# Two more pairs of gate tiles in seven products, and an earlier place for two copies and one load

## The chip, the cores and the metric

The kernel runs on one core of a Trainium2 chip. The metric is device time in microseconds (us) of one execution; smaller is better. A core has five instruction queues that run side by side: TensorE (PE in the profile, with PEld for its weight loads), VectorE (DVE), ScalarE (ACT), GpSimd (POOL) and SyncE (SP, which here only issues DMAs). Each queue runs its instructions in the order in which the program gives them to it, and waits at an instruction until what it needs is there.

## The reference, cut to what matters

Two layers over 512 tokens of width 1024, ahead of which 16 learned tokens are put. In float32:

```
h = RMSNorm(x)
[u_pool | z_pool | c_q | c_kv | k_rope | z_mla | g_pool | g_mla] = h @ W_in    # 512,512,768,256,32,512,1024,1024 columns
y_pool = W_pool_up( PoolMix(u_pool) * silu(z_pool) )      # four groups: mean of the last 2, 4, 8, 16, then 128x128 weights a group
y_mla  = W_mla_up( MLA(c_q, c_kv, k_rope) * silu(z_mla) ) # causal attention, 8 heads
x = x + W_out( sigmoid(g_pool) * y_pool + sigmoid(g_mla) * y_mla )
```

g_pool and g_mla are 1024 columns each: eight output tiles of 128, called gp and gm here. After the second layer the 16 learned tokens are dropped, so that layer computes its gates for 512 tokens only.

## The kernel before, in words

**Data and precision.** Activations lie transposed, channels on the 128 partitions and tokens along the free dimension. Each float32 operand is split in a high and a low part, and each product is three matmuls, high x high (line L192 of the profile), low x high (L195) and high x low (L196), into one PSUM bank. Output tile m of a product with 1024 inputs is 8 blocks of 128 rows, so 24 matmuls; its weights are two half tiles of 128x512 (256 KB). Each half tile is fetched by SP into one of three buffers `raw` (L115); ScalarE copies the high part (`whi`, L187) and VectorE subtracts to get the low part (`wlo`, L188), each into one of three buffers. So three half tiles are in flight at a time.

**Seven products for eight.** In the second layer the pairs gp0 to gp3 are computed as a 2x2 block product with seven products for eight (a scheme of Strassen's kind): the blocks are the two output tiles, two halves of 512 inputs and two halves of 256 tokens. Sums of the four blocks of weights are made ahead, during the first layer, by DMA: SP copies a half tile into DRAM (`weight_sums`, L356), and POOL adds others onto it by accumulating DMAs (L359). Sums of the activations (`mixed`) are made once. `fast` runs the products in the order 1, 6, 7, 5, 2, 4, 3, each with 4 blocks x 3 matmuls of 256 columns, and VectorE combines them (`fast` L632 to L647). `got_gp` then takes the gate's tanh on ScalarE and multiplies the pooled values by it on VectorE. The other gates, gm0 to gm7, go through `add` as plain products of 512 columns; `ev_gate` takes their tanh, and a DMA puts them into DRAM (`gate`). The output product W_out uses seven products as well (`out_pairs`, L1092 on): there product 6 adds onto the PSUM bank of product 1, so it waits until ScalarE has carried product 1 away (`carry`, L1163); POOL adds that to x by an accumulating DMA.

**What sets the order.** A list `plan` holds the matmul work that fills the gaps of the attention heads. A generator `stream` emits it, and fetches a half tile's weights when their predecessors are three tiles ahead. `fill` advances the plan by FILL ns of matmul time for each gap (2950 in the first layer, 2700 in the second) until the name in RESERVE is reached; what is left runs after the heads. `after(ns, f)` calls f when the plan's clock has come so far. A scheduler then orders each engine's instructions; `behind(a, b)` makes it put a behind b. The pooled groups' weights (128x512, `wgr`) are planned after `v`, fetched into a `raw` buffer like the rest, and split by `split` into the two `sv` buffers (L303 and L304).

**The change and the prediction's steps touch** `wload`, `weight_sums`, `fast`, `got_gp`, `carry`, the plan, and the constants FILL and RESERVE.

## Time and profile before

| what | us |
|---|---|
| median of 3 runs (781.44 to 783.92) | 782.54 |
| the profiled execution | 781.9 |
| its span | 780.1 |
| TensorE busy | 773.2 |
| VectorE busy | 569.7 |
| ScalarE busy | 444.7 |
| POOL busy | 232.7 |
| granted TensorE clock | 1.00 |

Engine rows read: start, length, engine, line, operation, outputs <- inputs, shape, count; in square brackets how long the engine had been idle, and what released it. Group rows give the busy time, the mean of one in ns, and the idle time of the engine ahead of the group. The stretch from 608 to 690 us lies in the second layer's heads. Idle time of an engine that TensorE does not wait for costs nothing.

### The profile page before, as it was taken

The page shows a single profiled execution, that of the slowest core. Times are in us where ns is not written, and L with a number is a line of the kernel's source. Part 1 is how long each engine was busy: PE and PEld are TensorE (multiplying, and loading weights), DVE is VectorE, ACT ScalarE, POOL GpSimd, SP SyncE. Part 2 cuts the span into 40 slices and gives each one's busy share as a digit, 9 for nine tenths or more (in the row PEclk, how much of TensorE's full clock was granted, in tenths as well). Part 3 has the DMA queues.
Part 4 walks back from the last instruction along what each step waited for, and adds up shares of the span by engine and source line. Part 5 has one row for each costly group of instructions (what it writes and reads, how often), then busy time and mean ns, then how long its engine had stood idle before and what let it go on. Part 6 is the DMA issues. An engine that isn't in the chain of part 4 may idle for free.

```text
span 780.1 us, 15325 instructions
## 1 busy us (share of the span) xinstructions
PE 773.2 (99%) x5469; PEld 710.9 (91%) x5469; DVE 569.7 (73%) x1326; ACT 444.7 (57%) x1016; POOL 232.7 (30%) x303
## 2 busy tenths in 40 slices
PE   9999999999999999999999999999999999999998
PEld 8999899999999999999997898887788999988887
DVE  5848787446778876589764577866897888864994
ACT  7645555645566665645564446546657766664552
POOL 1024525103335333211330136221006625340213
PEclk9999999999999999999999999999999999999999
DMA  6232457765646465565662424425557666662645
GB/s 245 82 96 89 125 171 151 177 168 144 156 110 164 116 141 120 156 156 184 169 171 82 109 75 122 133 62 178 146 132 167 173 187 158 175 226 72 210 137 154
DMA packets 65325, 112.92 MB, mean 145 GB/s; under 512 B 10704, under 2 KB 15696, under 8 KB 65248
## 3 DMA queue, kind: packets, MB, share of 16 engines
q1 hardware_dynamic: 55344, 92.18, 39.1%
q0 software_dynamic: 8896, 17.92, 12.9%
q10 hardware_dynamic: 1008, 1.84, 0.7%
q8 instruction: 43, 0.70, 0.4%
q14 instruction: 34, 0.28, 0.1%
HBM read 100.18 MB, written 22.62 MB: 157 GB/s over the span
## 4 chain that ended last, share of the span: by engine, by line
PE 91%; DVE 4%; DMA 2%; ACT 1%; issue 1%; POOL 0%; DVEq 0%; ACTq 0%; POOLq 0%
PE mm L192 26%; PE mm L196 26%; PE mm L195 25%; PE S L195 3%; PE S L196 3%; PE S L192 3%; PE mm L979 2%; DVE wlo L188 1%; PE o L985 1%; PE o L984 1%; PE S L506 1%; DMA raw<-wgr 1%; DMA xb<-xT 1%; PE mm L408 1%; ACT whi L187 0%
## 5 line engine op out<-in xcount | busy, mean ns | idle before, releaser
L192 PE MATMUL mm<-hh,whi 128*128 128x264 f32 (+2 forms) x992 | 306.2, 311 | 0.5 <-DVE u L550 0.4
L196 PE MATMUL mm<-hh,wlo 128*128 128x264 f32 (+2 forms) x992 | 304.4, 309 | 0.1
L195 PE MATMUL mm<-hl,whi 128*128 128x264 f32 (+2 forms) x992 | 304.1, 308 | 0.0
L188 DVE TENSOR_TENSOR wlo<-raw,whi 128x512 fp32r<-128x512 f32 (+1 forms) x253 | 180.0, 714 | 100.3 <-ACT whi L187 98.0
L187 ACT ACTIVATE whi<-raw 128x512 fp32r<-128x512 f32 (+1 forms) x253 | 154.2, 613 | 168.7 <-PE mm L195 110.2
L192 PEld LDWEIGHTS mm<-hh,whi 128*128 128x128 f32 x992 | 186.2, 188 | 11.3 <-issue 1.0
L195 PEld LDWEIGHTS mm<-hl,whi 128*128 128x128 f32 x992 | 186.8, 188 | 8.7
L196 PEld LDWEIGHTS mm<-hh,wlo 128*128 128x128 f32 x992 | 185.9, 188 | 9.0 <-DVE wlo L188 0.6
L922 POOL TENSOR_SCALAR pa<-pa,rs 128x272 f32<-128x272 f32 (+1 forms) x32 | 33.2, 1038 | 103.3 <-DVE rs L941 64.5
L922 POOL TENSOR_SCALAR cq<-cq,rs 128x400 f32<-128x400 f32 (+1 forms) x32 | 51.2, 1600 | 0.0
L192 PE MATMUL mm<-cq,whi 128*128 128x264 f32 (+2 forms) x140 | 43.8, 313 | 0.0
L195 PE MATMUL mm<-cq,whi 128*128 128x264 f32 (+2 forms) x140 | 43.7, 312 | 0.0
L196 PE MATMUL mm<-cq,wlo 128*128 128x264 f32 (+2 forms) x140 | 43.3, 312 | 0.1
L908 DVE CUSTOM_DVE_ANT_0 S<-S,maskw,nqs 128x272 f32<-128x272 f32 (+4 forms) x80 | 38.6, 498 | 5.3 <-PE S L196 5.0
L725 POOL TENSOR_TENSOR racc<-racc,tmp 128x264 f32<-128x264 f32 (+1 forms) x15 | 14.0, 936 | 85.5 <-ACT tmp L724 85.5
L304 DVE TENSOR_TENSOR tl<-mm,th 128x512 fp32r<-128x512 f32 (+1 forms) x64 | 30.0, 483 | 8.0 <-ACT th L303 6.3
L359 POOL DMA_DIRECT2D wsum<-wout x8 | 7.0, 875 | 91.6 <-PE mm L196 86.9
L303 ACT ACTIVATE th<-mm 128x512 fp32r<-128x512 f32 (+1 forms) x64 | 26.3, 433 | 10.2 <-PE mm L979 9.6
L915 ACT ACTIVATE cq<-S,bia 128x400 f32<-128x400 f32 (+2 forms) x48 | 24.5, 514 | 13.2 <-DVE bia L953 8.5
L192 PE MATMUL mm<-u,whi 128*128 128x264 f32 (+1 forms) x96 | 31.3, 326 | 0.0
L196 PE MATMUL mm<-u,wlo 128*128 128x264 f32 (+1 forms) x96 | 30.9, 322 | 0.0
L195 PE MATMUL mm<-kn,whi 128*128 128x264 f32 (+1 forms) x96 | 30.6, 320 | 0.0
(344 smaller groups left out, 1684.7 us busy)
## 6 DMA issues: line engine op xcount, KB each, us to landing
raw<-win SPq DMA_DIRECT2D x139, 256.0 KB, 2.8
raw<-wout SPq DMA_DIRECT2D x22, 256.0 KB, 3.6
bc<-kdr SPq DMA_DIRECT2D x16, 264.0 KB, 4.5
wsum<-wout SPq DMA_DIRECT2D x16, 256.0 KB, 3.5
raw<-wpu SPq DMA_DIRECT2D x16, 256.0 KB, 2.7
wsumgp<-win SPq DMA_DIRECT2D x16, 256.0 KB, 3.4
raw<-wmu SPq DMA_DIRECT2D x16, 256.0 KB, 2.8
raw<-wsumgp SPq DMA_DIRECT2D x16, 256.0 KB, 4.3
```

What stands on the lines that cost most here:

```text
L187: act.activation(hi[:, :n], raw[:, :n], AF.Copy)
L188: dve.tensor_sub(lo[:, :n], raw[:, :n], hi[:, :n].bitcast(F32))
L192: first = pe.matmul(out, wh, xh, start=start, stop=False, skip_group_check=more)
L195: pe.matmul(out, wh, xl, start=False, stop=False, skip_group_check=more)
L196: newest[0] = pe.matmul(out, wl, xh, start=False, stop=stop, skip_group_check=more)
L303: act.activation(hi[:, a:b], src, AF.Copy)
L304: dve.tensor_sub(lo[:, a:b], src, hi[:, a:b].bitcast(F32))
L725: self.acc_last = gp.tensor_add(self.acc[:, a:b], self.acc[:, a:b], t[:, :b - a])
L908: dve.tensor_tensor_reduce(out=sv, in0=sv, in1=mask, scale=nqs[:, i, h:h + 1], scalar=3e38, op0=ALU.add, op1=ALU.min, accum_out=bia[:, c:c ...
L915: act.activation(pv, sv, AF.Exp, scale=-1.0, bias=bia[:, i:i + 1], accum_out=rs[:, c:c + 1])
L922: gp.tensor_scalar(pt[i], pt[i], rs[:, i:i + 1], None, op0=ALU.mult)
L979: pe.transpose(tr[:, P * (i - j):P * (i - j + 1)], pt[i][:, NM + P * j:NM + P * (j + 1)], ident)
```

## The change

Three things are done, beside constants.

1. Of layer 1's eight gm tiles, gm2 with gm3 and gm4 with gm5 become the pairs gq1 and gq2, by `fast`, with the weight sums `wsum["gm"]`, which are made like those of gp: eight steps a pair in the first layer, 64 instead of 48, 3100 ns apart instead of 3850. `got_gm` takes the tanh of each 256-token half on ScalarE and sends each half to DRAM by a DMA of ScalarE's own queue. The order of layer 1's gates was gm0, gm1, gp0, gm2, gp1, gm3, gp2, gm4, gp3, gm5, gm6, gm7; it is gm0, gm1, gp0, gq1, gp1, gp2, gq2, gp3, gm6, gm7. FILL of layer 1 goes from 2700 to 2640, RESERVE from gm5 to gp3.
2. After a carry is emitted, the second and the third weight copy that follow it in the program (`urgent`) are put behind it on ScalarE.
3. The pooled groups' weights are fetched into a buffer `bc` of their own kind, not into `raw`, and are planned after `u2`, not after `v`.

```
-FILL = (2950.0, 2700.0)
-RESERVE = ("gm5", "gm5")
+FILL = (2950.0, 2640.0)
+RESERVE = ("gm5", "gp3")
...
     loads = [0]
+    urgent = []
 
     def wload(src, n, gain, spare, buf=None, held=False):
+        if held:
+            hi, lo = slot("sv", F32R, bufs=2), slot("sv", F32R, bufs=2)
+            raw = slot("bc", bufs=3)
+            sp.dma_start(raw[:, :n], src)
+            split(hi, lo, raw[:, :n], 0, n)
+            return hi, lo
...
-        if held:
-            hi, lo = slot("sv", F32R, bufs=2), slot("sv", F32R, bufs=2)
-            split(hi, lo, raw[:, :n], 0, n)
-            return hi, lo
...
-        act.activation(hi[:, :n], raw[:, :n], AF.Copy)
+        made = act.activation(hi[:, :n], raw[:, :n], AF.Copy)
+        for e in urgent:
+            e[1] += 1
+            if 1 < e[1] < 4:
+                behind(made, e[0])
...
-    def weight_sums(name, w):
+    def weight_sums(name, w, u0=0):
...
-        def fast(self, name, a, b, u, got):
+        def fast(self, name, a, b, s, u, got):
             order = (1, 6, 7, 5, 2, 4, 3)
-            s = wsum["gp"][u]
...
+        def got_gm(self, m, s, v, t):
+            if self.gms[m] is None:
+                self.gms[m] = slot("ts" if m % 2 else "tc")
+            d = self.gms[m][:, s[0]:s[1]]
+            act.activation(d, v, AF.Tanh, scale=0.5)
+            act.dma_start(gate[:, m, s[0] - NM:s[1] - NM], d)
...
-                act.activation(t, v, AF.Copy, scale=scale)
+                urgent.append([act.activation(t, v, AF.Copy, scale=scale), 0])
                 gp.dma_start(xb[:, m, s[0]:s[1]], t, accum_op=ALU.add)
...
+                if m == 2:
+                    add("yw", wgr[l], 512, body=self.hold)
+                    plan[-1].held = True
...
-            add("yw", wgr[l], 512, body=self.hold)
-            plan[-1].held = True
...
-                for e in ("gm0", "gm1", "gp0", "gm2", "gp1", "gm3", "gp2", "gm4", "gp3", "gm5", "gm6", "gm7"):
+                for e in ("gm0", "gm1", "gp0", "gq1", "gp1", "gp2", "gq2", "gp3", "gm6", "gm7"):
...
+                    elif e[:2] == "gq":
+                        self.fast(e, wi(MT_GM + 2 * m), wi(MT_GM + 2 * m + 1), wsum["gm"][m], m, self.got_gm)
...
-                sums = [*weight_sums(0, [wout[0, m] for m in OUT]), *weight_sums("gp", [win[1, MT_GP + m] for m in range(8)])]
+                sums = [*weight_sums(0, [wout[0, m] for m in OUT]), *weight_sums("gp", [win[1, MT_GP + m] for m in range(8)]),
+                        *weight_sums("gm", [win[1, MT_GM + m] for m in range(6)], 1)]
                 for i, fn in enumerate(sums):
-                    after(3850 * (i + 1), fn)
+                    after(3100 * (i + 1), fn)
```

What this does to the order of instructions stands in three places. Lines of the changed kernel are some 7 to 13 higher than those of before for the same statement (L190 is before's L187, L199 is L192, L403 is L396, L1176 is L1163).

At the start of SP's queue, before (xb takes the rows of x, raw the first weights):

```order
L126 DMA xb<-xT 128x528
L144 DMA xb<-xT 128x1056
L148 DMA raw_157<-win 128x512
L144 DMA xb<-xT 128x1056
L148 DMA raw_160<-win 128x512
L144 DMA xb<-xT 128x1056
```

and of the change:

```order
L126 DMA xb<-xT 128x528
L178 DMA bc_1082<-wgr 128x512
L144 DMA xb<-xT 128x1056
L148 DMA raw_160<-win 128x512
L144 DMA xb<-xT 128x1056
L148 DMA raw_163<-win 128x512
L144 DMA xb<-xT 128x1056
```

The pooled groups' weights of the first layer, which were the 43rd entry of this queue, are now the 5th, ahead of six of x's eight rows of blocks.

ScalarE in the second layer's output product, before (S are the banks of product 1 and 6, sv the carried results, kh, kl and raw the fetched weights):

```order
L303 ACTIVATE sq_9839<-cq_1856_9557 128x256
L187 ACTIVATE whi_10125<-raw_10123 128x512
L1163 ACTIVATE sv_10036<-S_10023 128x256
L1163 ACTIVATE sv_10058<-S_10045 128x256
L303 ACTIVATE rinv_9843<-cq_1876_9627 128x256
```

and of the change:

```order
L310 ACTIVATE rinv_10000<-cq_1904_9784 128x256
L1176 ACTIVATE sv_10193<-S_10180 128x256
L1176 ACTIVATE sv_10215<-S_10202 128x256
L190 ACTIVATE whi_10220<-kl_10218 128x512
L190 ACTIVATE whi_10241<-raw_10239 128x512
```

The copies that stood ahead of the first two carries stand behind them. In the first layer's output product the same is seen of the change:

```order
L403 ACTIVATE cq_1007_5692<-xb 128x528
L1176 ACTIVATE sv_5499<-S_5486 128x264
L1176 ACTIVATE sv_5521<-S_5508 128x264
L190 ACTIVATE whi_5526<-kl_5524 128x512
L190 ACTIVATE whi_5547<-raw_5545 128x512
L190 ACTIVATE whi_5568<-kh_5566 128x512
```

where before the copies from kl, raw, kh and raw for the next products stood ahead of these two carries.

More of the change, by code (lines that the diff above doesn't have):

```diff
@@ L336, in trunk @@
     kdr = [dp.tile([H, T], F32, name=f"kdr{l}") for l in range(DEPTH)]
-    wsum = {n: [dp.tile([P, 4, 512], F32, name=f"wsum{n}{u}") for u in range(k)] for n, k in (("gp", 4), (0, 2), (1, 2))}
+    wsum = {n: [dp.tile([P, 4, 512], F32, name=f"wsum{n}{u}") for u in range(k)] for n, k in (("gp", 4), ("gm", 3), (0, 2), (1, 2))}
     gate = dp.tile([P, 6, SEQ], F32, name="gate")
@@ L359, in add @@
             behind(gp.dma_start(d, src[1], accum_op=ALU.add), earlier(4000))
-        for u in range(len(w) // 2):
+        for u in range(u0, len(w) // 2):
             for fn, i in ((copy, 0), (copy, 2), (add, 0), (copy, 1), (add, 2), (add, 1), (copy, 3), (add, 3)):
@@ L1265, in register @@
             if self.last:
-                for e in ("gm0", "gm1", "gp0", "gm2", "gp1", "gm3", "gp2", "gm4", "gp3", "gm5", "gm6", "gm7"):
+                for e in ("gm0", "gm1", "gp0", "gq1", "gp1", "gp2", "gq2", "gp3", "gm6", "gm7"):
                     m = int(e[2])
                     if e[:2] == "gp":
-                        self.fast(e, wi(MT_GP + 2 * m), wi(MT_GP + 2 * m + 1), m, self.got_gp)
+                        self.fast(e, wi(MT_GP + 2 * m), wi(MT_GP + 2 * m + 1), wsum["gp"][m], m, self.got_gp)
+                    elif e[:2] == "gq":
+                        self.fast(e, wi(MT_GM + 2 * m), wi(MT_GM + 2 * m + 1), wsum["gm"][m], m, self.got_gm)
                     else:
```

## The prediction, made before the changed kernel was timed

> **What bounds the kernel now.** I read the page first, then windows of the stages that the change touches, then the timeline around each wait.
>
> ```profile
> span 780.1 us, 15325 instructions
> PE 773.2 (99%) x5469; PEld 710.9 (91%) x5469; DVE 569.7 (73%) x1326; ACT 444.7 (57%) x1016; POOL 232.7 (30%) x303
> PE 91%; DVE 4%; DMA 2%; ACT 1%; issue 1%; POOL 0%; DVEq 0%; ACTq 0%; POOLq 0%
> ```
>
> TensorE is busy for 99% of the span and makes 91% of the chain that ended last, so an instruction taken off TensorE shortens the run, as long as its operands still come in time. The profiled execution took 781.9 us, 1.8 around its span; the median of the three runs is 782.54 (781.44 to 783.92), 0.64 above it. Sums below are made against 781.9. I count 0.3% of the median, 2.35 us, as what a measurement of this kernel can tell from no change.
>
> The averages hide that the second layer's attention, where the changed products are filled in, is far tighter on VectorE (columns: window, length, then busy time and count of PE, PEld, DVE, ACT, POOL, then clock, DMA share, GB/s):
>
> ```profile
> 608.00:690.00 82.00, 81.91 (x595) 76.82 (x594) 73.20 (x186) 57.75 (x150) 38.31 (x46) 1.00 0.68 184
> 640.00:660.00 20.00, 19.93 (x140) 18.28 (x139) 17.64 (x46) 13.82 (x38) 10.80 (x13) 1.00 0.67 163
> 720.00:740.00 20.00, 20.00 (x88) 16.20 (x87) 19.11 (x33) 9.79 (x17) 4.41 (x8) 1.00 0.60 189
> 740.00:760.00 20.00, 18.93 (x118) 16.81 (x117) 18.86 (x45) 11.89 (x29) 3.53 (x5) 1.00 0.47 146
> ```
>
> From 608 to 690 TensorE lacks 0.09 us of 82, VectorE 8.8, ScalarE 24. The granted clock is 1.00 throughout.
>
> **The products.** A plain pair of gate tiles is 2 tiles x 8 blocks x 3 matmuls = 48 of 512 columns; seven products are 7 x 4 x 3 = 84 of 256. The spacing of each, from the first and last row of an undisturbed series (7 and 9 rows):
>
> ```profile
> 644.73 0.40 PE L196 MATMUL mm<-hh,wlo 128*128 128x512 f32 x1
> 646.13 0.39 PE L196 MATMUL mm<-hh,wlo 128*128 128x512 f32 x1
> 615.01 0.28 PE L192 MATMUL mm<-sq,whi 128*128 128x256 f32 x1
> 615.96 0.29 PE L196 MATMUL mm<-sq,wlo 128*128 128x256 f32 x1
> ```
>
> 1.40/6 = 0.233 us and 0.95/8 = 0.119 us. A plain pair costs 48 x 0.233 = 11.20, seven products 84 x 0.119 = 9.98: 1.22 less, and two pairs -2.44.
>
> A rule speaks against this. The Trainium skill, page "TensorE: Matmul & The Clock Gate", section "Back-to-back issue gap", gives a sustained spacing of about 131 ns at 512 columns and 81 ns at 128. With an estimate of 92 ns at 256, drawn from that page's two figures, the pair would go from 6.3 to 7.7 us, two pairs +2.9 instead of -2.44, and the change would be slower. The trace disagrees: 233 ns and 119 ns stand there, nearer to that section's isolated formula (N/2.4 + 2.5 ns), so I give the rule no chance.
>
> **The wait for the pooled groups' weights.** They are loaded late, through a buffer that weights queue for:
>
> ```profile
> 79.42 2.87 DMA raw<-wgr
> 82.32 0.63 ACT L303 ACTIVATE sv<-raw 128x512 fp32r<-128x512 f32 x1 [2.28 <-DMA raw<-wgr]
> 83.58 0.40 PE L196 MATMUL mm<-whi,kl 128*128 128x512 f32 x1
> 84.38 0.50 PE L192 MATMUL mm<-whi,kh 128*128 128x512 f32 x1 [0.41 <-DVE u L550]
> 476.03 0.40 PE L196 MATMUL mm<-whi,kl 128*128 128x512 f32 x1
> 476.48 0.50 PE L192 MATMUL mm<-whi,kh 128*128 128x512 f32 x1
> ```
>
> ScalarE stood 2.28 us for that load, and the copies and subtractions behind it were late: TensorE starts 0.80 after the row before instead of 0.23, so 0.57 is lost, and 0.22 in layer 1. Both go: -0.79. What could take their place is VectorE's multiplication for u, which the row names; bounds 0 to -0.79. I take it all, since the copy that delayed it stands elsewhere now.
>
> But the scheduler puts the load of the first layer, 256 KB, on SP's queue behind the second xb load, ahead of the first two-row xb load. There it is early and in the way:
>
> ```profile
> 3.62 0.33 SPq L144 DMA_DIRECT2D xb<-xT  x1
> 2.00:4.00 2.00, 2.00 (x12) 2.00 (x11) 0.00 (x0) 1.02 (x3) 1.60 (x6) 1.00 0.86 319
> 4.00:6.00 2.00, 1.91 (x8) 1.50 (x8) 1.59 (x4) 1.79 (x4) 0.00 (x0) 1.00 1.01 328
> 8.42 1.36 ACT L389 ACTIVATE hh<-xb,gn 128x528 fp32r<-128x528 f32 x2 [1.55 <-DMA xb<-xT]
> 9.21 0.39 PE L192 MATMUL S<-hh,whi 128*128 128x264 f32 x1 [0.25 <-ACT hh L389]
> ```
>
> At 328 GB/s 256 KB (262,144 bytes) take 0.80 us of engines that are already full, and both ScalarE and TensorE wait there for the xb rows. Up to 0.28 us (0.14 of the window from 2 to 4) of free DMA time can take some of it: +0.5 to +0.8, I take +0.6. In layer 1 the load goes out before the first layer's last head is through, beside loads with room; I take 0, at worst the 0.22 that its wait was worth.
>
> **ScalarE's order at the end.** In the output product the second pass over a PSUM bank waits until ScalarE has carried the first result away; ScalarE stood with a weight copy ahead of it that waited for a free buffer:
>
> ```profile
> 754.52 0.28 PE L196 MATMUL S<-hh,wlo 128*128 128x256 f32 x1
> 755.73 0.28 PE L196 MATMUL mm<-hh,wlo 128*128 128x256 f32 x1
> 756.12 0.63 ACT L187 ACTIVATE whi<-raw 128x512 fp32r<-128x512 f32 x1 [1.57 <-PE mm L196]
> 756.66 0.64 ACT L1163 ACTIVATE sv<-S 128x256 f32<-128x256 f32 x2
> 757.08 0.39 PE L192 MATMUL S<-cq,whi 128*128 128x256 f32 x1 [1.07 <-ACT sv L1163]
> ```
>
> TensorE starts at 757.08, 1.35 after the row before instead of 0.12: 1.23 lost. With the two carries first, they can run from 754.80 (754.52 + 0.28) to 755.34 (0.27 apart), and the copy that is now behind them ends near 755.97; with some 0.2 for each of two releases between engines, as the rows' gaps show (756.66 + 0.27 to 757.08 is 0.15), TensorE goes at about 756.4 where it would be ready at 755.85. So 0.55 to 0.57 of the wait stays, under another name: -0.66, bounds 0 and -1.23.
>
> The first layer has the same turn without such a wait today, because the copies that it needs stand ahead of the carries:
>
> ```profile
> 378.75 0.63 ACT L187 ACTIVATE whi<-raw 128x512 fp32r<-128x512 f32 x1
> 379.29 0.65 ACT L1163 ACTIVATE sv<-S 128x264 f32<-128x264 f32 x2
> 379.83 0.65 ACT L396 ACTIVATE cq<-xb 128x528 f32<-128x528 f32 x1
> ```
>
> Afterwards the four copies that stood ahead of the carries stand behind them, the first of which holds the weights of the pass that waits for the carry. By the working above it would be 0.55 late, at worst two copies (2 x 0.54 = 1.1, the spacing from 378.75 to 379.29); at best it fits before TensorE asks. I take +0.3. Behind the copies on ScalarE only squares and further copies queue.
>
> **The attention's supply.** Each new pair reads seven half tiles, not four: per pair three more loads, copies and VectorE subtractions, and five VectorE combinations that were not there. The rows of such instructions, and of the loads from 597 to 690:
>
> ```profile
> L188 DVE TENSOR_TENSOR wlo<-raw,whi 128x512 fp32r<-128x512 f32 x34 | 23.8, 700 | 4.7 <-ACT whi L187 4.3
> 643.21 0.67 DVE L188 TENSOR_TENSOR wlo<-raw,whi 128x512 fp32r<-128x512 f32 x1
> 643.80 0.41 DVE L638 TENSOR_TENSOR sv<-sv,mm 128x256 f32<-128x256 f32 x1
> 644.13 0.41 DVE L658 SCALAR_TENSOR_TENSOR xb<-tmp,xb 128x256 f32<-128x256 f32 x1
> 643.93 0.50 PE L196 MATMUL mm<-hh,wlo 128*128 128x512 f32 x1
> raw<-win SPq DMA_DIRECT2D x21, 256.0 KB, 3.4
> raw<-wsumgp SPq DMA_DIRECT2D x15, 256.0 KB, 4.2
> ```
>
> Starts follow at 0.59 and 0.33 us, less than the durations. For two pairs VectorE gets 6 x 0.59 + 10 x 0.33 = 6.8 us more; ScalarE 6 x 0.63 = 3.8, the copies of the first product and four more DMA issues, within its 24 idle. VectorE then needs 73.2 + 6.8 = 80.0, and the stretch is to shrink to 82 - 2.44 = 79.6. That can't be. The subtraction at 643.21 ended at 643.88 and TensorE used it at 643.93, so there is no lead left at the end of such a pair even now. If nothing is wasted, 0.4 us is lost; at the 95.6% of 720 to 740, at which TensorE still ran full, 80.0/0.956 = 83.7, +4.1. Work can slide behind 690, since the fourth pooled pair and two plain gates are now kept for after the heads: with 2.5 us of it there, 77.5/0.956 = 81.1, +1.5. I take +1.5, between 0 and 4.1.
>
> Loads go from the 36 of these two rows to 42 in some 90 us, one per 2.1; a landing of 3.4 to 4.2 with three buffers in flight allows one per 1.1 to 1.4. Nothing is added for them.
>
> **The sums in layer 0.** Eight more loads of 256 KB on SP, eight adding ones on POOL, spaced 3.1 us instead of 3.85: SP's and POOL's queues have room (POOL 30%), and 0 is taken, 1 at worst if the second layer's start waits for a queue.
>
> **Sum.** -2.44 - 0.79 + 0.6 - 0.66 + 0.3 + 1.5 = -1.49: 780.4 from 781.9, 781.05 on the median. I say 780.7.
>
> **Rivals.** *A: nothing is taken back in the attention.* VectorE's combinations fit, its queue is elastic, the first layer's copies are in time: -1.49 - 1.5 - 0.3 = -3.3, 778.6 (779.2 on the median). For it: at 95.6% from 720 to 740 TensorE lost nothing. Against: the 80.0 in 79.6.
>
> *B: VectorE becomes the bound from 608 to 690.* Nothing slides, and its share stays at the 94.3% of 740 to 760: 80.0/0.943 = 84.8, +5.3 instead of +1.5: +2.3, 784.2 (784.9 on the median); at 93% it is 786.0. It decides, slower, as soon as VectorE can't pass 94.3%. For it: the row from 640 to 660, in the middle of this attention, shows 88%. Against: chains of short instructions elsewhere go higher.
>
> *C: the gains are eaten by smaller things.* The new subtractions collide with POOL's work. In one place, beside POOL's L668, this subtraction takes long, in another not:
>
> ```profile
> 76.97 1.19 DVE L188 TENSOR_TENSOR wlo<-raw,whi 128x512 fp32r<-128x512 f32 x1
> 77.57 1.54 POOL L668 TENSOR_TENSOR tmp<-u 128x542 f32<-128x542 f32 x1
> 637.80 0.67 DVE L188 TENSOR_TENSOR wlo<-raw,whi 128x512 fp32r<-128x512 f32 x1
> ```
>
> If all six met it at 1.19 instead of 0.67, VectorE would need 3.1 more; at 0.956 that is +3.3, so +1.8, 783.7 (784.3 on the median); with half of them +0.1, 782.0 (782.7). The Trainium skill, page "SBUF — State Buffer", section "SBUF: two separate sides", has the rule: a VectorE instruction with two SBUF inputs and a POOL instruction that reads SBUF exclude one another, for the whole instruction. The mean of 700 ns over 34 in the stretch, with POOL busy for 38 of 82 us, speaks for few such meetings there.
>
> **Chances.** Forecast 0.46 (its own range 779.4 to 782.2: faster 0.2 of it, as the attention's cost falls below 0.6, the same 0.26), A 0.22 (faster), C 0.18 (the same), B 0.14 (slower). Faster 0.42, same 0.44, slower 0.14. The range reaches from within A, 778.3, into B's lower half, 784.2.
>
> **What would show it.** TensorE's row count falls in 512-column and rises in 256-column matmuls by 96 and 168. Right: no ACT wait on the wgr load near 82, PE's first xb wait near 9.2 later by 0.6, the wait at 757 shortened to about half with the copy L187 as its releaser, VectorE at 95% or more from 608 to 688 with 1 to 2 us of PE idle there. Wrong: PE idle of less than 0.3 in that stretch (A), or over 4 with VectorE below 95% (B); or a new idle of over 1 us at the layers' boundary (390 to 400) or in the first output product, which I have at 0 and 0.3.

## The result: 1.6% slower

The changed kernel takes 796.3 us (median of 4 runs, 794.09 to 796.99), against 782.02 for the kernel before (4 runs): a ratio of 1.0163, 95% interval 1.0139 to 1.0187. The forecast was 780.7, its range ended at 784.2; the kernel is 12 us beyond it. The profiled execution of the changed kernel took 796.99.

The page of the changed kernel (span; busy time, share and count of each engine; shares of the chain that ended last):

```profile
span 795.2 us, 15546 instructions
PE 778.8 (98%) x5541; PEld 716.6 (90%) x5541; DVE 576.4 (72%) x1342; ACT 449.2 (56%) x1028; POOL 237.1 (30%) x311
PE 75%; DMA 7%; DVE 7%; issue 6%; ACT 3%; POOL 2%; SPq 0%; DVEq 0%; POOLq 0%; ACTq 0%
```

TensorE has the 72 matmuls more that were announced (168 of 256 columns in, 96 of 512 out). Its busy share fell by a point only, but its share of the chain fell from 91% to 75%: it now waits for others. For whom, its waits tell (engine, what it wanted, line <- engine and line that released it: us in total, times, longest). The first rows of the whole run's list, without one of the start that the kernel before has too:

```profile
PE o L997 <- ACT th L310: 2.0, 4, 0.9
PE S L199 <- ACT cq L928: 2.0, 1, 2.0
PE mm L199 <- ACT whi L190: 1.6, 1, 1.6
PE mm L199 <- ACT q L310: 0.9, 1, 0.9
PE S L199 <- ACT kh L310: 0.8, 2, 0.4
PE S L203 <- DVE wlo L195: 0.8, 1, 0.8
```

Only two of these six are waits for weights (`whi`, `wlo`). Three are waits for the attention heads: `cq` is the exponential, `th` its high part, `kh` the keys. `q` is the high part of the heads' finished output; that wait stands in the first layer, where the product after the attention reads it. The list of the kernel before begins so, and holds nothing of that kind:

```profile
PE S L192 <- ACT sv L1163: 1.1, 1, 1.1
PE wps L137 <- DVE na L842: 1.0, 1, 1.0
```

Where the time went is read from the lag of one and the same TensorE instruction, its start in the changed kernel's profile less its start in that of before. The same is given for the kernels of the experiments below, each from one profiled execution; the points are four instructions that stand at 360, 600, 720 and 776.63 us in the kernel before (in the first layer's end, ahead of the second layer's heads, behind them, and the last matmul).

| kernel | 360 | 600 | 720 | 776.63 | heads: 600 to 720 |
|---|---|---|---|---|---|
| the change | +2.9 | +3.5 | +13.1 | +14.7 | +9.5 |
| pairs | +2.5 | +2.6 | +12.9 | +13.0 | +10.3 |
| pairs_2660 | +0.3 | +0.2 | +11.9 | +11.8 | +11.6 |
| pairs_2620 | +0.2 | +0.2 | +4.6 | +5.4 | +4.5 |
| few_loads | +1.2 | +1.9 | +6.1 | +6.0 | +4.2 |
| sums_only | +1.3 | +1.6 | +3.1 | +3.7 | +1.5 |
| urgent | 0.0 | +0.6 | +1.1 | +1.8 | +0.5 |
| wgr | 0.0 | -0.2 | +0.6 | +0.9 | +0.8 |
| before_2640 | -1.1 | +0.1 | +0.6 | +0.9 | +0.5 |
| before_held | -0.2 | +1.4 | +9.0 | +9.0 | +7.6 |

One execution differs from another: before_2640 has the first layer of the kernel before, unchanged, and is 1.1 us ahead of it at 360. So a lag below some 1.2 us in the first layer is no evidence. The 9.5 us in the heads are: that is two thirds of the loss, although the products there became 2.44 us cheaper. `pairs` has TensorE's order of the change in the heads and +10.3 there, so a second execution of one order agrees within a microsecond.

Windows of the changed kernel (window, length, busy time and count of PE, PEld, DVE, ACT, POOL, clock, DMA share, GB/s):

```profile
8.00:12.00 4.00, 4.00 (x23) 4.00 (x22) 3.31 (x6) 3.31 (x7) 0.00 (x0) 0.57 1.04 408
611.00:702.00 91.00, 84.56 (x650) 80.46 (x649) 76.50 (x188) 60.65 (x151) 32.33 (x41) 0.98 0.63 170
620.00:630.00 10.00, 9.69 (x79) 9.23 (x78) 9.72 (x25) 7.67 (x23) 6.55 (x8) 1.00 0.65 185
630.00:640.00 10.00, 9.61 (x76) 9.09 (x76) 9.71 (x29) 6.48 (x17) 0.56 (x2) 1.00 0.62 180
656.00:660.00 4.00, 3.50 (x30) 3.25 (x28) 2.42 (x8) 1.48 (x5) 0.82 (x1) 1.00 0.82 206
660.00:667.00 7.00, 3.90 (x21) 2.79 (x22) 6.79 (x19) 6.40 (x18) 3.41 (x4) 1.00 0.62 149
667.40:670.60 3.20, 3.20 (x14) 3.01 (x14) 2.27 (x10) 0.00 (x0) 0.76 (x2) 0.50 0.08 29
```

Over the heads (611 to 702) VectorE is busy for 76.5 of 91 us, 84%. It is not short of time on average. It is full from 620 to 640, where TensorE lacks 0.7 of 20 us, and once more behind a gap: from 656 to 660 ScalarE does 1.48 of 4 us and VectorE 2.42, and then both are nearly full to 667, while TensorE does 3.9 of 7. The timeline of that place (start, length, engine, line, operation, outputs <- inputs; in brackets the idle time before it and its releaser):

```profile
655.52 0.27 PE L992 MATMUL mm<-cst,cq 128*128 128x128 f32 x1
658.52 0.63 ACT L190 ACTIVATE whi<-raw 128x512 fp32r<-128x512 f32 x1 [3.55 <-DMA raw<-wsumgp]
659.06 0.58 ACT L928 ACTIVATE cq<-S,bia 128x400 f32<-128x400 f32 x1
659.63 0.27 ACT L310 ACTIVATE th<-mm 128x128 fp32r<-128x128 f32 x1
659.16 0.28 PE L203 MATMUL mm<-hh,wlo 128*128 128x256 f32 x1
659.95 0.33 PE L997 MATMUL o<-th,vt 128*128 128x128 f32 x1 [0.50 <-ACT th L310]
661.77 0.39 PE L199 MATMUL S<-kh,qhl 128*128 128x272 f32 x1 [0.38 <-ACT kh L310]
662.84 0.40 PE L202 MATMUL S<-kl,qhl 128*128 128x272 f32 x1 [0.68 <-DVE kl L311]
665.71 0.45 PE L199 MATMUL S<-kh,qhl 128*128 128x400 f32 x1 [2.01 <-ACT cq L928]
668.74 0.41 PE L199 MATMUL mm<-cq,whi 128*128 128x256 f32 x1
668.96 0.41 PE L202 MATMUL mm<-cq,whi 128*128 128x256 f32 x1
```

ScalarE's queue had the copy of a half tile ahead of a head's exponential (`cq`) and high part (`th`). The half tile's load was late, and ScalarE stood 3.55 us with work behind it that was not about weights: the last matmul for `th` had run at 655.52. From 659.16 to 668.74 TensorE's own order holds only the heads' products, no gate tile, so each of the late steps (`th`, `kh`, `kl`, `cq`) is a TensorE wait. After these waits the matmuls of 256 columns follow at 0.22 us instead of 0.12, at a granted clock of 0.50, up to 670.6.

The load itself is slow, and the queues show what it ran beside (SP's issues, three in one row, then POOL's adding DMA for the weight sums of this layer's output product):

```profile
652.49 3.28 SPq L115 DMA_DIRECT2D raw<-wsumgp  x3
652.55 0.90 POOL L366 DMA_DIRECT2D wsum<-wout  x1 [5.48 <-PE mm L203]
```

The first of the three was issued at 652.49, and the copy that waited for it starts at 658.52, 6.0 us later; the prediction's rows have medians of 3.4 and 4.2. The kernel before has such a meeting too. There the adding DMA, issued at 648.78, and a load issued at 649.67 took, to landing:

```profile
wsum<-wout POOLq DMA_DIRECT2D x1, 256.0 KB, 7.6
raw<-win SPq DMA_DIRECT2D x1, 256.0 KB, 6.8
```

TensorE lost 0.09 us in the whole stretch from 608 to 690 all the same. A half tile lasts a plain product 12 x 0.233 = 2.80 us and a pair of seven products 12 x 0.119 = 1.43, while three buffers at 6.0 us each supply one per 2.0. That this difference turns a harmless meeting into a costly one is worked out from these rows; no run isolates it. The wait itself comes again with both pairs: ScalarE stands for `raw<-wsumgp` between 658 and 659.2 for 2.53 us in `pairs`, 2.43 in `pairs_2660`, 2.03 in `pairs_2700` and 1.28 in `pairs_2620`, each time 6 to 8 us behind the issue of that adding DMA.

### The profile page after: what moved, and what is told of

Same layout as the page of the kernel before. It is cut to its first block, busy times and chain, and to the rows that moved or that the text cites. A ratio compares the mean times of both kernels' runs of the same rounds, so it can differ in the third digit from the quotient of the medians.

```text
span 795.2 us, 15546 instructions
## 1 busy us (share of the span) xinstructions
PE 778.8 (98%) x5541; PEld 716.6 (90%) x5541; DVE 576.4 (72%) x1342; ACT 449.2 (56%) x1028; POOL 237.1 (30%) x311
## 4 chain that ended last, share of the span: by engine, by line
PE 75%; DMA 7%; DVE 7%; issue 6%; ACT 3%; POOL 2%; SPq 0%; DVEq 0%; POOLq 0%; ACTq 0%
PE mm L199 21%; PE mm L203 21%; PE mm L202 21%; DVE wlo L195 3%; PE mm L992 2%; PE S L203 2%; PE S L202 2%; PE S L199 2%; DMA raw<-wsumgp 2%; DMA raw<-wqb 1%; DMA raw<-win 1%; DMA raw<-wsumgm 1%; ACT whi L190 1%; PE o L998 1%; PE o L997 1%
## 5 line engine op out<-in xcount | busy, mean ns | idle before, releaser
L199 PE MATMUL mm<-hh,whi 128*128 128x264 f32 (+2 forms) x984 | 301.3, 309 | 3.0 <-ACT whi L190 1.6
L203 PE MATMUL mm<-hh,wlo 128*128 128x264 f32 (+2 forms) x984 | 299.2, 306 | 0.2 <-DVE wlo L195 0.2
L202 PE MATMUL mm<-hl,whi 128*128 128x264 f32 (+2 forms) x984 | 298.4, 304 | 0.0
L195 DVE TENSOR_TENSOR wlo<-raw,whi 128x512 fp32r<-128x512 f32 (+1 forms) x259 | 185.1, 718 | 111.1 <-ACT whi L190 109.4
L190 ACT ACTIVATE whi<-raw 128x512 fp32r<-128x512 f32 (+1 forms) x259 | 157.5, 613 | 178.8 <-PE mm L202 99.3
L199 PEld LDWEIGHTS mm<-hh,whi 128*128 128x128 f32 x984 | 185.0, 189 | 13.8 <-ACT whi L190 3.6
L203 PE MATMUL mm<-cq,wlo 128*128 128x264 f32 (+2 forms) x156 | 48.5, 313 | 0.1
L199 PE MATMUL mm<-cq,whi 128*128 128x264 f32 (+2 forms) x156 | 48.6, 311 | 0.0
L202 PE MATMUL mm<-cq,whi 128*128 128x264 f32 (+2 forms) x156 | 48.5, 311 | 0.0
L921 DVE CUSTOM_DVE_ANT_0 S<-S,maskw,nqs 128x288 f32<-128x288 f32 (+4 forms) x80 | 38.6, 499 | 3.5 <-PE S L203 3.3
L738 POOL TENSOR_TENSOR racc<-racc,tmp 128x264 f32<-128x264 f32 (+1 forms) x15 | 14.3, 953 | 86.6 <-ACT tmp L737 78.2
L203 PEld LDWEIGHTS mm<-cq,wlo 128*128 128x128 f32 x156 | 29.8, 191 | 2.4 <-DVE wlo L195 0.7
L199 PEld LDWEIGHTS mm<-cq,whi 128*128 128x128 f32 x156 | 29.8, 191 | 1.6
L199 PE MATMUL mm<-u,whi 128*128 128x264 f32 (+1 forms) x96 | 31.3, 326 | 0.0
L202 PEld LDWEIGHTS mm<-cq,whi 128*128 128x128 f32 x156 | 29.8, 191 | 1.6
```

The costliest lines, as they stand in the source:

```text
L190: made = act.activation(hi[:, :n], raw[:, :n], AF.Copy)
L195: dve.tensor_sub(lo[:, :n], raw[:, :n], hi[:, :n].bitcast(F32))
L199: first = pe.matmul(out, wh, xh, start=start, stop=False, skip_group_check=more)
L202: pe.matmul(out, wh, xl, start=False, stop=False, skip_group_check=more)
L203: newest[0] = pe.matmul(out, wl, xh, start=False, stop=stop, skip_group_check=more)
L738: self.acc_last = gp.tensor_add(self.acc[:, a:b], self.acc[:, a:b], t[:, :b - a])
```

## The experiments

The expectations go by letters for some theories: N, the added work itself costs time where supply is tight; D, any new drawing of the order costs time, whatever is added; O, the heads' products come in a stretch without fillers, and holding the heads back behind fillers would close the hole. In diffs, `pairs` is the kernel of the first experiment.

### The three parts alone

Part 1 alone (`pairs`: the new products, their sums, FILL and RESERVE as in the change's diff), part 2 alone (`urgent`), part 3 alone (`wgr`).

```
pairs:  -FILL = (2950.0, 2700.0)  +FILL = (2950.0, 2640.0)
        -RESERVE = ("gm5", "gm5") +RESERVE = ("gm5", "gp3")
        +  got_gm, "gq1", "gq2", weight_sums("gm", ..., 1), after(3100 * (i + 1), fn)
urgent: +  urgent.append([carry, 0]); behind(made, e[0]) for the 2nd and 3rd copy after it
wgr:    +  if held: raw = slot("bc", bufs=3) ...; planned after u2
```

> Part 1 alone: the two new pairs with their weight sums, FILL 2640 and RESERVE gp3; the carries and the pooled groups' weights as before. The changed kernel is 14 us slower than the one before; by the places where TensorE stands in its trace, this part costs 9 to 12 us of it (some 12 us of waits in the second layer's attention, less 2.3 saved). Theory O (the order of the heads and the filling products on TensorE): 791 to 794, with a stretch near 655 to 665 in which TensorE runs 3.5 us of head matmuls without a filling matmul among them and waits for the softmax. Theory V (VectorE is the bound): the same time, but VectorE at 95% or more over the whole stretch from 610 to 700. Theory of the other parts (copies and the early load cost it all): 780 to 781.

> Part 2 alone: the second and third weight copy after a carry stand behind it. My prediction: -0.66 at the end and +0.3 in the first layer, 781.7. From the changed kernel's trace: waits of 0.6 near 382 and about 2.1 us in the last output product in place of the 1.38 of before: 783 to 784.5.

> Part 3 alone: the pooled groups' weights early and through bc. My prediction: -0.79 + 0.6, 781.8. From the changed kernel's trace: about 2 us lost at the start, as the load goes ahead of the second half of the first weights, and the half clock that follows the wait; 0.5 to 0.8 won back at the two old waits: 783 to 783.6.

| part | median, us | before | ratio (95%) | difference |
|---|---|---|---|---|
| pairs | 795.25 | 782.41 | 1.0157 (1.0119 to 1.0196) | +12.8 |
| urgent | 785.38 | 782.41 | 1.0035 (1.0022 to 1.0048) | +3.0 |
| wgr | 783.13 | 782.41 | 1.0017 (1.0003 to 1.003) | +0.7 |

No part gains. `wgr` lies within its expected range, `urgent` 0.9 above its own, and `pairs` 1.3 above theory O's; theory V is out, as VectorE is busy for 75.76 of 91 us, 83%, in the row below. The sum of the three is 16.5, the whole change 14.3; nearly all of it is part 1. Its loss in the heads is that of the change (+10.3 in the table), with the same signs in other places: in the windows of `pairs` the clock is down to 0.83 where TensorE lacks 3.25 us.

```profile
611.00:702.00 91.00, 84.30 (x647) 80.86 (x645) 75.76 (x189) 59.89 (x151) 29.96 (x41) 0.96 0.62 168
650.00:670.00 20.00, 16.75 (x112) 15.77 (x110) 16.20 (x46) 10.94 (x29) 6.51 (x8) 0.83 0.58 135
```

`urgent` does what was said at the end: the carries stand first, and the wait of 1.07 us for `sv` in the kernel before is gone. Its timeline there:

```profile
755.03 0.66 ACT L1174 ACTIVATE sv<-S 128x256 f32<-128x256 f32 x2
759.16 0.39 PE L197 MATMUL S<-cq,whi 128*128 128x256 f32 x1 [0.23 <-ACT whi L188]
```

Yet in its profile the two output products lose 0.6 us (first layer) and 0.7 us (second). The matmul order changed in both with the copies' order, and the remaining delays are many of 0.1 to 0.5 us. (This profile is of the fastest of its ten executions, 783.89.) The heads lose 0.5, though their matmuls stand in the same order as before.

### Where the heads go in: FILL

```
-FILL = (2950.0, 2640.0)
+FILL = (2950.0, 2620.0)     pairs_2620; also 2660 and 2700
```

> Part 1 alone as in the run pairs, but with FILL of the second layer 2620 instead of 2640, which changes where the heads' matmuls stand among the filling ones: the 3.5 us stretch of head matmuls alone is gone from TensorE's order (the longest in that region is 1.55 us of matmul work), the work and the loads are the same. Theory O: 4 to 8 us faster than the run pairs, 785 to 789. Theory V: VectorE's load is the same, so within 1.5 us of the run pairs.

> Part 1 alone with the FILL of before, 2700. TensorE's order has no stretch of heads alone as long as with 2640 (the longest in the second half of the attention 1.87 us of matmul work). Theory O: well below the run pairs (795.3), near pairs_2620: 786 to 789. Theory V: 794 to 796.

> Part 1 alone with FILL 2660; the draws with pairs so far are 787.6 (2620), 792.6 (2700) and 795.3 (2640). Theory D: anywhere from 782 to 796. Theory N: 787 to 795, not below 786.

787.64 (before 782.41; 1.0067, 1.0047 to 1.0087) at 2620, 796.67 (783.19; 1.0179, 1.0138 to 1.022) at 2660, 792.63 (783.17; 1.0116, 1.0084 to 1.0148) at 2700. With 795.25 at 2640, four orders of the same work lie up to 9 us apart, and none reaches the kernel before. Theory O foresaw 2620, not the others: 792.63 is in neither range given for 2700, and 796.67 is above all that was expected for 2660. Then the same knob without the new pairs:

> The kernel before, FILL of the second layer 2640 instead of 2700, nothing else; the work is the same to the instruction, only the order of heads and fillers differs. Theory D (every new order of this stretch is a new draw, and the one of before was a good one): 786 to 794. Theory N (the new work of the pairs costs the 10 us): 782 to 784.5.

> The kernel before with FILL 2680. Theory D: 785 to 793. Theory N: 782 to 784.5.

> The kernel before with FILL 2720. Theory D: 785 to 793. Theory N: 782 to 784.5.

782.95, 783.49 and 785.77, against 783.19 for its own 2700 (ratios 1.0002, 0.9991 to 1.0014; 1.0007, 0.9996 to 1.0018; 1.0031, 1.0018 to 1.0045). The first two lie in theory N's range, 785.77 in D's. With this knob a new order by itself costs 0 to 2.6 us, where the same knob with the pairs gave 5.2 to 13.5. That speaks for N, but does not exclude D: `before_held` below is a new order without any new work that costs 8.0.

At 2620 the longest wait is another one. The first row of TensorE's list and the windows of `pairs_2620`:

```profile
PE mm L192 <- DVE sv L646: 1.7, 1, 1.7
```

```profile
608.00:692.00 84.00, 79.56 (x623) 75.62 (x622) 75.04 (x186) 59.38 (x151) 36.04 (x45) 1.00 0.67 175
650.00:670.00 20.00, 18.29 (x147) 17.65 (x146) 19.68 (x54) 14.05 (x38) 8.12 (x10) 1.00 0.66 154
```

Here VectorE is full for 20 us (19.68) and the wait is for its combination of a pair's products; the clock stays at 1.00. Over the 84 us it is busy for 89%.

### VectorE's combinations, and the spacing of the sums

`no_combos` is `pairs_2620` without the ten combinations of the two new pairs: the gate takes four of the products as they are, so it leaves out part of the reference's work. `sums_3850` is `pairs_2620` with the old spacing of the sums, `one_pair` has gq2 only, with all the sums.

```
no_combos: + elif name[:2] == "gq":
           +     if p in (2, 3, 4, 5):
           +         got(2 * u + (p > 3), XH[0 if p in (2, 4) else 1], ps, ps)
sums_3850: - after(3100 * (i + 1), fn)   + after(3850 * (i + 1), fn)
one_pair:  + "gm0", "gm1", "gp0", "gm2", "gp1", "gm3", "gp2", "gq2", "gp3", "gm6", "gm7"; FILL 2680
```

> The run pairs_2620 with VectorE's ten combinations of the two new pairs left out: the gate takes four of the products as they are, so the output is not the reference's. Loads, matmuls and ScalarE's work stay. The run pairs_2620 is 5.2 us over the kernel before, with 6.5 us of TensorE waits from 620 to 680, the longest (1.9 us) behind such a combination. Theory V2 (locally, VectorE's queue is late with the combinations, and the PSUM banks that they free hold TensorE up): 4 us or more below pairs_2620, 780 to 783.5. Theory O2 (the rest too is only where heads and fillers stand): within 2 us of pairs_2620, 785.6 to 789.6.

> The run pairs_2620 with the 64 steps of the weight sums spaced 3850 ns instead of 3100. In pairs_2620 a weight load near 331 landed 0.85 us later than before beside an adding DMA of POOL, and TensorE waited 1.06 instead of 0.23. If that is a matter of spacing: 0.8 less, 786.8. If the sums collide somewhere wherever they stand: 787 to 788.5.

> Part 1 with one of its two pairs: gq2 by seven products, gm2 and gm3 plain between the pooled pairs as before (gm0, gm1, gp0, gm2, gp1, gm3, gp2, gq2, gp3, gm6, gm7), FILL 2680, all the sums. Theory V2 (VectorE can't serve neighbouring pairs of seven products): half or less of the waits of pairs_2620, 783 to 785. Theory O2: it depends on where heads and fillers stand; TensorE's order has no stretch of heads alone over 1.7 us of matmul work here, so 781.5 to 783.

Against 783.17: no_combos 789.9 (1.0084, 1.0067 to 1.0102), sums_3850 790.18 (1.009, 1.0069 to 1.0111), one_pair 787.69 (1.0062, 1.0042 to 1.0083). All three are above every range that was expected for them. Taking the combinations away gains nothing against `pairs_2620` (1.0067); since their place in the order moves other work too, this excludes them as the main cause, not as a small one. The old spacing doesn't help either: in its profile the lag at 360 is only 0.1, where the close spacing had put waits, but 2.1 us are lost between 360 and 600, where its last sums now run. Its order in the heads is that of `pairs_2620`, and so is its loss there: +5.0 against +4.5. One pair, with all the sums, costs 4.5 us.

### Holding the heads back

```
-            nqs, hold = self.nqs, h == 0
+            nqs, hold = self.nqs, h == 0 or self.last
held2:  -  hold=hold and i == 1)   +  hold=hold and i == 1 or self.last and i == 3)
```

This makes the score products of every head of the second layer wait in the order until the filler ahead is through (held_2640, in `pairs`; before_held, in the kernel before); `held2` does it for a second group of scores as well.

> The run pairs (795.3) with one more dependency: in the second layer each head's first score matmul stands behind the last filling matmul that was written ahead of it, as was so for head 0 alone. No work is added; TensorE's order loses its 3.5 us stretch of heads alone (longest 1.6 us). Theory O (the scheduler put the heads ahead of fillers whose weights the chip had long ready): 783 to 787. Theory W (weights, copies or VectorE are really late, and the heads ran ahead for that reason): TensorE then waits for the weights instead, 793 to 797.

> As held_2640, and each head's second group of scores also stands behind the fillers written ahead of it. Theory O: the head's two halves are spread as written, so as held_2640 or up to 2 us less, 781 to 786. Theory W: 793 to 797.

> Control: the kernel before with the dependency of held_2640. Its attention loses some 0.5 us to waits from 608 to 690, so nothing can be won: within 1 us of before by either theory. If it is faster by over 1.5 us, the dependency does something else than theory O says.

> As held2_2640 with FILL 2700 (the run pairs_2700 had 792.6). TensorE's order has no stretch of heads alone of over 1.5 us in the second half. Theory O: as held2_2640, 780.5 to 785, and the number FILL loses its weight. Theory W: 790 to 795.

Against 782.71: held_2640 796.74 (1.0178, 1.0162 to 1.0193), held2_2640 803.89 (1.0262, 1.0238 to 1.0287), held2_2700 798.15 (1.0189, 1.0163 to 1.0215), before_held 790.75 (1.0103, 1.0087 to 1.0118). Held heads are no better with the pairs; without them, where 1 us at most was expected, they are 8 us worse. The waits then are for heads that are late themselves; the first row of TensorE's list of held_2640:

```profile
PE o L990 <- DVE tmp L1006: 4.7, 2, 4.1
```

So theory O in this form falls: the stretch without fillers was not cured by holding heads back. It also shows how narrow the place of the heads is in the kernel before: one line that adds no work, and draws TensorE's order of heads and fillers anew, costs it 8 us.

### Fewer weights to fetch and split

`few_loads` is `pairs` (FILL 2640) where the products 6, 5 and 4 in each new pair use the weights of the product ahead of them: the same matmuls and combinations, but 4 of 7 half tiles a pair are loaded, copied and split, as many as a plain pair has. Its gates are not the reference's.

```
+            kept = [None]
+                w = kept[0] = w or kept[0]
-            plan.append(Gemm((self.l, name), [src[p] for p in order], ...
+            plan.append(Gemm((self.l, name), [None if name[:2] == "gq" and p in (6, 5, 4) else src[p] for p in order], ...
```

> The run pairs (795.3) with four of seven half tiles loaded, copied and split in each new pair, as many as its two plain tiles needed; products 6, 5 and 4 use the weights of the product ahead of them, so the output is not the reference's. TensorE's matmuls, VectorE's combinations and ScalarE's gates stay, and TensorE's order still has its stretch of heads alone (3.4 us of matmul work). Theory S (the supply of weights: six loads, copies and splits more, in queues that the heads' softmax shares): 780 to 786. Theory P (the seven products in themselves, or that stretch of heads): 791 to 796.

788.5 against 782.63: 1.0074 (1.0051 to 1.0096), where `pairs` had 1.0157 (1.0119 to 1.0196). The intervals don't overlap, and the time lies between the ranges of theories S and P. With six loads, copies and subtractions less, about 7 of `pairs`' 12.8 us are gone (795.25 - 788.5 = 6.75, in other words 12.8 - 5.9), and in the profiles 6.1 of them lie in the heads: +4.2 there, not +10.3.

This does not price the six loads. With them the scheduler also drew the order of heads and fillers anew: TensorE's order in this trace leaves that of `pairs` at about 630 us. Four orders with all the loads lie 9 us apart, and the best of them, `pairs_2620` at 787.64 and +4.5 in the heads, is as fast as `few_loads`. So the 7 us are the loads' and the new order's together; how much is the loads', no run tells. The longest wait of `few_loads`:

```profile
PE S L192 <- ACT cq L924: 2.1, 1, 2.1
```

The order still has a stretch of heads alone, with a wait of 2.1 us for the exponential. What ScalarE does ahead of its weight copies is in these groups: count, busy time, mean ns, idle time ahead of them and what ended it, in the heads of the kernel before, of `pairs`' best order `pairs_2620` and of `few_loads` (608 to 692, before up to 690) and of the change (608 to 692):

```profile
L187 ACT ACTIVATE whi<-raw 128x512 fp32r<-128x512 f32 x34 | 21.4, 630 | 13.7 <-PE mm L195 7.1 <-DMA raw<-win 2.7 <-DMA raw<-wsumgp 2.4
```

```profile
L187 ACT ACTIVATE whi<-raw 128x512 fp32r<-128x512 f32 x38 | 24.0, 631 | 18.8 <-PE mm L195 8.0 <-DMA raw<-win 3.8 <-DMA raw<-wsumgp 3.3
```

```profile
L187 ACT ACTIVATE whi<-raw 128x512 fp32r<-128x512 f32 x32 | 20.2, 631 | 19.4 <-PE mm L195 12.8 <-DMA raw<-wsumgm 2.8 <-DMA raw<-wsumgp 1.3
```

```profile
L190 ACT ACTIVATE whi<-raw 128x512 fp32r<-128x512 f32 x35 | 22.1, 631 | 24.1 <-PE mm L202 8.2 <-DMA raw<-wsumgp 5.2 <-DMA raw<-win 3.9
```

Before, ScalarE stood 13.7 us ahead of 34 copies, 0.40 for one; in the change 24.1 ahead of 35, 0.69 for one. Whatever stands ready behind such a copy, as a head's exponential did at 658.52, stands too. Waits for loads (`raw<-...`) make 5.1 of it before, 9.1 in the change, 7.1 in `pairs_2620` and 4.1 in `few_loads`. But this idle time is no measure of the loss: `few_loads` has 0.61 ahead of a copy, `pairs_2620` 0.49, and they take the same time.

### The sums alone

The kernel before with the 16 more steps of the sums, 3100 ns apart, and no new pair that would use them.

```
+  *weight_sums("gm", [win[1, MT_GM + m] for m in range(6)], 1)
-  after(3850 * (i + 1), fn)   +  after(3100 * (i + 1), fn)
```

> The kernel before with the 16 more steps of weight sums and the 3100 ns spacing, but without the pairs that would use them; the second layer's order stays as it was. My prediction had 0 for the sums, 1 at worst. From the traces: 0.8 to 1.5 us near 334, some 0.5 near 452: 783.5 to 785.5. If the sums cost nothing by themselves: 782 to 783.3.

786.67 against 783.04: 1.005 (1.003 to 1.007), +3.6 us (2.3 to 5.5 by the interval). That is above its range; the sums do cost time by themselves. One place carries 1.0 of it. Its timeline, and behind it the rows that answer in the kernel before:

```profile
325.52 0.84 POOL L359 DMA_DIRECT2D wsumgm<-wsumgm  x1 [6.16 <-PE mm L1038]
332.23 1.15 ACT L187 ACTIVATE whi<-raw 128x512 fp32r<-128x512 f32 x2 [1.85 <-DMA raw<-wmu]
335.40 0.51 PE L192 MATMUL mm<-q,whi 128*128 128x264 f32 x2 [1.09 <-ACT q L303]
```

```profile
329.27 0.81 POOL L359 DMA_DIRECT2D wsumgp<-win  x1 [8.68 <-PE mm L196]
330.98 1.16 ACT L187 ACTIVATE whi<-raw 128x512 fp32r<-128x512 f32 x2 [0.82 <-DMA raw<-wmu]
```

The copy waits 1.85 us for its load instead of 0.82, and the heads' output (`q`) behind it on ScalarE comes 1.09 late for TensorE. The load was in flight together with the adding DMA of 325.52, which took 5.4 us to land, to about 330.9. Before, the adding DMA ahead of it was issued at 319.70 and landed 6.3 us later, and the next, at 329.27, starts when the load is nearly in. The place tells the same in all traces. In the twelve kernels with sums 3100 ns apart, which have one order of matmuls there, the copy waits 1.62 to 2.29 us and TensorE 0.86 to 1.53; in the eight others, `sums_3850` among them, the copy waits 0.73 to 0.92 and TensorE at most 0.16.

One profile's lag is a poor measure of the rest, since executions differ. At 360 us the eleven kernels that differ from the kernel before by these sums alone, up to there, lag by 0.2 to 3.4, 1.65 on the mean; the four in which the first layer is unchanged are 0.2 to 1.1 ahead. So some 2 us of the sums' price lie in the first layer. The other places in the profile are 0.7 near 150, 0.3 near 452, 1.5 in the second layer's heads and 0.6 in the last product; in the last two none of the added sums runs and TensorE's order is that of before, so what they owe to the edit isn't settled.

No kernel of these beats the one before. The best order with the pairs, `pairs_2620`, is 5.2 behind it, 4.5 of them in the heads by its profile: even there the 2.44 of the products does not arrive.

## Why the prediction was wrong, step by step

**The products: right in what they save.** The spacing after is 0.12 at 256 columns, the 72 matmuls are as counted. But -2.44 is a gain only if the operands come in time. The step's estimate of 92 ns at 256 columns, for the rule that it set aside, is not on the straight line between the two figures that it names, which gives 98; the measured 119 rules out both.

**The wait for the pooled groups' weights: half right.** The waits of 0.57 and 0.22 are gone: the rows of the first layer in `wgr`, which follow at 0.23, and no wait near 480 in the change. The +0.6 for the load at the head of SP's queue was of the right size alone (the profile of `wgr` has +0.55 at its start; its other gains and losses leave +0.7 on the median), and too small in the change's profile, +1.94 behind the start. The wait moved to another load than the step had it at: not the first two-row xb load, but the second half of the first weights. Start of the changed kernel:

```profile
2.58 0.43 SPq L178 DMA_DIRECT2D bc<-wgr  x1
6.83 0.63 ACT L190 ACTIVATE whi<-raw 128x512 fp32r<-128x512 f32 x1 [1.58 <-DMA raw<-win]
7.51 0.39 PE L199 MATMUL mm<-hh,whi 128*128 128x264 f32 x1 [1.58 <-ACT whi L190]
10.28 0.42 PE L203 MATMUL S<-hh,wlo 128*128 128x264 f32 x1
10.50 0.42 PE L202 MATMUL mm<-hl,whi 128*128 128x264 f32 x1
```

After that one wait the clock is 0.57 from 8 to 12 us, and the matmuls of 264 columns follow at 0.22. That a wait could cost more than itself had no term.

**The carries: wrong sign.** -0.66 + 0.3 = -0.36 was summed; part 2 alone costs 3.0 (1.7 to 3.8 by its interval). The step priced the one wait that it took away. It did not price what else moves when copies, their subtractions and the matmuls that use them are drawn in a new order. In the change TensorE waits 0.91 us (1.03 from start to start, less 0.12) for a subtraction that stands on VectorE behind an addition to x:

```profile
775.09 0.42 DVE L1172 SCALAR_TENSOR_TENSOR xb<-mm,xb 128x256 f32<-128x256 f32 x1 [1.39 <-issue]
775.44 0.68 DVE L195 TENSOR_TENSOR wlo<-kl,whi 128x512 fp32r<-128x512 f32 x1
775.14 0.28 PE L203 MATMUL S<-cq,wlo 128*128 128x256 f32 x1
776.17 0.39 PE L203 MATMUL S<-cq,wlo 128*128 128x256 f32 x1 [0.75 <-DVE wlo L195]
```

VectorE stood 1.39 us ahead of the addition; the profile names no releaser, so that it was the accumulating DMA of a carried result, which is named at such an addition in the kernel before, is argued and not shown. `urgent` has no such wait, and still loses 3.0. There the loss is spread over delays of 0.1 to 0.5 us, and which of them belong to the edit stays open.

**The attention's supply: the step that failed.** +1.5, between 0 and 4.1, was taken from VectorE's share over the stretch: so much work, at 95.6%, so long a stretch. Measured in the profiles, the heads cost 9.5 us more in the change and 10.3 in `pairs`, with the 2.44 saved inside it, so 12 to 13 us of new waits. VectorE's added work was sized right (6.7 us more over the run, 6.8 in the step), but its share of the heads was 84%, not 95%.

What the step had wrong stands in its sentence on the loads: one per 2.1 us is needed, a landing of 3.4 to 4.2 with three buffers allows one per 1.1 to 1.4, so nothing is added for them. Both numbers are means over the stretch. At the place that TensorE paid for, a half tile took 6.0 us, and the pairs that now stand side by side use one per 1.43. "Its 24 idle" for ScalarE's copies failed there in kind: idle time of an in-order queue isn't room if it consists of standing at a copy whose load is late, with a head's exponential behind it. That this happened is shown, at 658.52. How much of these 12 to 13 us it makes is not: the same work in other orders costs 4.5 to 11.6 in the heads, `few_loads` changed loads and order together, and `before_held` shows that an order alone can cost 8. The cause of the size stays open between the supply and the order.

**The sums: mis-sized.** 0, at worst 1, was taken because the queues had room; 3.6 was measured, some 2 of it in the first layer, where the sums run. Room on the queue that issues is not room for the transfers beside which a weight load must land.

**The rivals.** B had the side right, slower, and the wrong mechanism: VectorE as the bound of the whole stretch at 94.3%. Its share is 84%. It is full in parts (97% from 620 to 640 and from 660 to 667 in the change, 98% from 650 to 670 in `pairs_2620`), and the most time is lost behind a gap in its own work. The sign that was given for B did come: TensorE is idle for 6.4 of 91 us with VectorE below 95%; but VectorE as the bound would have been above. A and C, with everything fitting or smaller collisions, are out: the subtractions of C take 705 ns on the mean of 38 in the change's heads, 700 on the mean of 34 before. The sign for the right rival stood in the prediction's own rows: TensorE lost 0.09 of 82 us, the subtraction at 643.21 came in with no lead, and the matmul work was arranged so. A stretch as tight as that had little to give, for six more half tiles or for another order.

**What stays open.** What the six loads cost in one and the same order of TensorE; a run of `few_loads` with the order of `pairs` held fast would tell, and one with the output product's sums taken out of the heads. Why 2620 and 2640 lie 7.6 us apart: the stretch of heads alone is a difference that the traces show, not one that a run isolated. And why `wgr`, `urgent` and `sums_only` each lose 0.5 to 1.5 us in heads whose TensorE order is unchanged; it can be the spread of single executions.

## What to carry to other kernels

When work is moved from a busy engine to engines with idle time, ask what that idle time is made of: on an in-order queue an instruction that waits for a DMA holds everything behind it, and if that is a softmax, TensorE pays. Price a change of supply by the waits at its tightest place (here 0.09 us of slack in 82), not by shares of a stretch, and price background transfers by the loads beside them. Run each part alone before trusting a sum: here three parts, each with a gain worked out for it, gained nothing alone. Where one constant moves the same work by 9 us, a variant that changes the order as well is not yet a price.

## What was not expected of the hardware

The granted clock fell to half after short waits. In the change it is 0.57 from 8 to 12 us, after one wait of 1.58 at 7.51; and 0.50 from 667.4 to 670.6, after waits of 0.50, 0.38, 0.68 and 2.01 us between 659 and 666, with TensorE busy for 3.9 of 7 us. The Trainium skill, page "TensorE: Matmul & The Clock Gate", section "HAM oscillation — how this bites in real kernels", names idle gaps of over about 3.4 us as what lowers it; here no single gap is so long, and the measurement decides. A shorter wait did not do it: `wgr` waits 0.78 us at the place of the 1.58, and its clock is 1.00 from 8 to 12. The fall costs: 14 matmuls from 667.4 to 670.6 take 3.2 us, by an estimate from the halved clock up to 1.6 more than at full speed.
